# A gated token mixer on one core: the third branch's weight sums issued without marks, and three ring slots with six raw blocks instead of four with four

## The chip, the core and the metric

The kernel runs on one core of a Trainium2 chip. The metric is the device time of one execution in microseconds (us). Times of single instructions come from one profiled execution, and are counted from the start of its span.

## What is computed

One layer on an input x of 512 positions by 1024 channels, in float32:

```python
h = rmsnorm(x, norm_mix)
p = h @ w_in                                   # 1024 x 6144
u, v, bg, cg, xb, zc, gl = split(p)            # six of 512 columns, gl of 3 x 1024
ya = sgu(gelu(u), gelu(v), ...)                # 512 columns each
yb = bg * causal_dwconv(cg * xb, conv_b_w)
yc = pool_mixer(zc, pool_w, pool_scale)
g = sigmoid(gl)                                # three gates
merged = g[0] * (ya @ w_br_a) + g[1] * (yb @ w_br_b) + g[2] * (yc @ w_br_c)
x = x + merged @ w_o                           # output projection
h = rmsnorm(x, norm_ffn)
ag, av = split(causal_dwconv(h @ w_up, ffn_conv_w))   # 2 x 2816 columns
x = x + (silu(ag) * av) @ w_down
return rmsnorm(x, norm_f)
```

## The kernel before, in words

**Matrix products.** Each float32 factor is split into a high and a low part, and a product is three matmuls: high by high (L81), high by low (L82) and low by high (L83), each of 128 x 128 by 128 x 512. `st` are the activations, `mv` the weights.

**Weights: raw buffers, cuts, ring.** Weights come in blocks of 512 KB, 128 partitions by 1024 columns. SyncE loads a block into a *raw* buffer (L106); `Raws.cap` says how many raw buffers may be filled at a time: 4. The pool `rawp` has eight tiles of this size; four are raw buffers, and four hold two of the ring's slots. A block is then *cut* into a slot of the ring, `ring_hi` by ScalarE (L59, or L63 with the sign turned) and `ring_lo` by VectorE (L67, or L64). After the cut the raw buffer is free and the next load is issued. The ring `own` has four slots (0 and 1 in the pool `act`, 2 and 3 in `rawp`). `Pieces` counts the pieces: piece j goes into slot j modulo the number of slots, and `take` makes the pieces ahead by as many as there are slots:

```python
def take(self, n=1):
    i = self.taken
    self.taken += n
    self.ahead(i + len(self.slots))
    return [self.slots[k % len(self.slots)] for k in range(i, i + n)]
```

So the number of slots says how early a cut stands in the order of the engines' instructions, too. A planner that works with costs of its own then settles the order of the instructions on each engine; the chip runs each engine's list in that order.

**Branches and gates.** For i = 0, 1, 2 the program does `branch(i)`, the product of ya, yb or yc with its weights, and `gate(i)`, the product of h with the gate's 1024 columns, the sigmoid, and the weighing of the branch's result with it. Both are done with seven products of quarters instead of eight (m1 to m7, a scheme like Strassen's). A branch has 7 products of 12 matmuls (one piece each, 84 matmuls), a gate 7 products of 24 (two pieces each, 168). Banks of TensorE are named bx, bd, ba in a branch and gx, gd, ga in a gate; bx and bd are added to further after ScalarE has copied what they hold (L951, into `bm...`, `m...`). VectorE adds and subtracts copies and banks (L842, `tt`), ScalarE applies the sigmoid (L961). After the three come the output projection (`po`), the second norm, whose transposed result is split into `h2T_hi` and `h2T_lo`, and the up projection with blocks ug and uv (`pug`, `puv`), which uses the ring through a class of its own, `Cols`, with four slots.

**Sums of weights.** The seven products need sums of a weight's quarters. Branches 0 and 1 make them with VectorE in the raw buffers (`add_branch`, L178): all four blocks of the branch, b11, b12, b22, b21, lie in raw buffers until the fourth to seventh product. The gates and branch 2 have them made by `WeightSums`: DMAs issued by GpSimd copy quarters to four buffers t1 to t4 in memory (L146) and add other quarters to them (L151, a DMA that accumulates); the blocks are then loaded from there (`g_t`, `br_t`). The sums of gates 0 and 1 are issued early, after `v_center`, without conditions. Those of branch 2 (`last_branch_sums`, eight DMAs of 512 KB) and of gate 2 (`gate_sums[2]`, eight of 1 MB) are paced by *marks*: `next_sum`, called after a product, has ScalarE copy one column of the product's bank (`mark`, L936), GpSimd copy that (`passed`, L407), and GpSimd issue the next DMAs of the list `behind`. GpSimd's instructions keep the order written. There are eleven marks: seven in gate 0, one in branch 1 and three in gate 1.

Of the kernel before, what the change touches and what calls it, by code (L numbers as in the profile page):

```python
# [8 lines left out]
F32R = mybir.dt.float32r  # L9
# [5 lines left out]
P = 128  # L15
# [11 lines left out]
def trunk_kernel(  # L27
# [8 lines left out]
    rawp = ctx.enter_context(tc.tile_pool(name="rawp", bufs=8))  # L36
# [83 lines left out]
    raws = Raws()  # L120
# [14 lines left out]
    class WeightSums:  # L135
        def __init__(self, name, b11, b12, b21, b22):
            t1, t2, t3, t4 = self.t = [
                dram.tile([P, b11.shape[1], 528], F32, name=f"{name}_t{i + 1}")[:, :, :512] for i in range(4)]
            self.base = [(t1, b11), (t3, b12), (t2, b22), (t4, b21)]
            self.added = [(t1, b12), (t3, b22), (t2, t1), (t4, t2)]  # L140

            self.products = {"m1": b11, "m2": b21, "m3": b22, "m4": t4, "m5": t1, "m6": t2, "m7": t3}

# [215 lines left out]
    slots = own  # L359
# [38 lines left out]
    def quarters(half, c0):  # L398
        return [half(k)[:, :, c0 + 512 * h:c0 + 512 * h + 512] for k in range(2) for h in range(2)]

    gate_sums = [WeightSums(f"g{i}", *quarters(lambda k: w_in_v[:, 4 * k:4 * k + 4], 3072 + 1024 * i))
                 for i in range(3)]
    last_branch_sums = WeightSums("br2", *quarters(lambda k: w_br_q[2][k], 0))
# [228 lines left out]
        v_gelu(t)  # L632
    v_center()
    pool_waits_for(pw_raw, "begun")
    for sums in gate_sums[:2]:
        sums.copy()
        sums.add()

# [164 lines left out]

    pieces = Pieces(slots)
    for i in range(3):
        if i < 2:
            add_branch(f"br{i}", *quarters(lambda k: w_br_q[i][k], 0), pieces)
# [74 lines left out]
    sums = []  # L884
# [39 lines left out]
    nc.vector.tensor_scalar(nrstd1, rstd1, -1.0, None, op0=ALU.mult)  # L924


    behind = [lambda: last_branch_sums.copy()]
    behind += [lambda: last_branch_sums.add(1)] * 4
    behind += [lambda: gate_sums[2].copy(2)] * 2
    behind += [lambda: gate_sums[2].add(1)] * 4  # L930

    def next_sum(o):
        if behind:
            n = len(behind)
            mark = tiny(f"mark{n}", f"mark{n}")
            nc.scalar.copy(mark, o[:, 0:1])  # L936
            pool_waits_for(mark, f"passed{n}")
            behind.pop(0)()
# [89 lines left out]
    def branch(i, form):  # L1028
        c = [[act.tile([P, S], F32, tag=f"m{8 + 2 * t + h}" if i == 0 else f"x{t}{h}", name=f"c{i}{t}{h}")
              for h in range(2)] for t in range(NT)]  # L1030
        x = banks(f"bx{i}")
        product(x, form("a11"), 2, True)
        m1 = copies(0, f"bm1{i}", x)
        d = banks(f"bd{i}")
        product(d, form("s1"), 2, True)
        m5 = copies(1, f"bm5{i}", d)
        product(x, form("s2"), 2, False)
        if i > 0:
            next_sum(x[1])
        m16 = copies(2, f"bm16{i}", x)  # L1040
        a = banks(f"ba{i}")
        product(a, form("a12"), 2, True)
        for r in range(2):
            tt(c[r][0], a[r], m1[r], ALU.subtract)
        product(x, form("s3"), 2, False)
        for r in range(2):
            tt(c[2 + r][1], x[r], m5[r], ALU.add)
        product(d, form("s4"), 2, False)
        for r in range(2):
            tt(c[r][1], d[r], m16[r], ALU.add)  # L1050
        product(x, form("a22"), 2, False)
        for r in range(2):
            nc.scalar.mul(c[2 + r][0], x[r], -1.0)
        return c
# [16 lines left out]
    def prepare2():  # L1071
        if ready:
            to_channels(*ready.pop(0), 1, h2, xr)

    for h in range(2):
        o = {}

# [46 lines left out]
        down_sums.copy(1)  # L1124
        down_sums.add(1)

    n = pieces.done % len(slots)
    assert pieces.done == pieces.taken
    slots = slots[n:] + slots[:n]
    blocks = Cols(col_blocks[n_in:], slots)  # L1130

    def up_conv(o, c, i, name):
# [129 lines left out]
    pieces = Pieces(slots)  # L1262
# [19 lines left out]
    x = banks("dx")  # L1282
# [38 lines left out]
    f = [[bank(f"df{r}{i}") for i in range(len(cuts[r]))] for r in range(2)]  # L1321
# [44 lines left out]
```

## Time and profile before

| | |
|---|---|
| median of 3 runs | 739.06 us (738.57 to 740.81) |
| profiled execution | 736.67 us |
| its span | 734.9 us |
| TensorE busy in the span | 720.7 us, 98% |
| VectorE | 562.7 us, 77% |
| ScalarE | 370.6 us, 50% |
| GpSimd | 62.6 us, 9% |

The span is the stretch from the first to the last instruction in the profile; the rest of the execution's time, 1.77 us, lies outside it. Busy shares are means over the whole span. In the rows below PE is TensorE's matmuls, PEld its weight loads, DVE VectorE, ACT ScalarE, POOL GpSimd, and SPq SyncE's DMA queue. An engine's row may be busy while it is not at its peak.

### The profile page before, as it was taken

Reading aid. Unit: us, or ns where it says so; the run is one execution under the profiler, and the core shown is the slowest. Engines: PE = TensorE matmul, PEld = TensorE weight load, DVE = VectorE, ACT = ScalarE, POOL = GpSimd, SP = SyncE. Lnnn points to the kernel's source line nnn. Section 1 sums busy time; section 2 is a strip of 40 time slices with the busy share of each in tenths; the row PEclk is TensorE's granted clock in tenths of the full one; section 3 lists DMA queues with packets and bytes.
Section 4 is the critical chain, followed back from the end, with each engine's and each line's share of the span. In section 5 each row is a group of like instructions: output and inputs, shape, how many; then the busy total and the mean of one; then the engine's idle time right before and its main releaser. Section 6 shows DMA issues by size and latency. Waiting matters only on the chain.

```text
span 734.9 us, 8928 instructions
## 1 busy us (share of the span) xinstructions
PE 720.7 (98%) x3258; PEld 594.8 (81%) x3258; DVE 562.7 (77%) x836; ACT 370.6 (50%) x551; POOL 62.6 (9%) x93
## 2 busy tenths in 40 slices
PE   8999999999999998999999999999999999999996
PEld 5888888888877886888888888888888888888885
DVE  6889899889598687677556786766787776997674
ACT  4744144266675565664444443443444444965453
POOL 0041210001221100000012010100000000000110
PEclk9999999999999999999999999999999999999999
DMA  8649999737999996675228999999633232576652
GB/s 254 192 170 283 244 331 237 183 90 232 304 313 313 229 295 199 196 225 183 87 75 264 236 296 285 253 311 220 178 97 105 86 106 82 155 234 201 194 163 114
DMA packets 89211, 150.87 MB, mean 205 GB/s; under 512 B 4008, under 2 KB 39248, under 8 KB 89168
## 3 DMA queue, kind: packets, MB, share of 16 engines
q1 hardware_dynamic: 68607, 96.76, 41.7%
q0 software_dynamic: 19840, 52.43, 29.8%
q10 hardware_dynamic: 720, 1.11, 0.4%
q8 instruction: 25, 0.41, 0.2%
q14 instruction: 19, 0.15, 0.1%
HBM read 148.20 MB, written 54.53 MB: 276 GB/s over the span
## 4 chain that ended last, share of the span: by engine, by line
PE 93%; DVE 3%; DMA 2%; ACT 1%; issue 1%; SPq 0%; ACTq 0%
PE pug L83 5%; PE puv L83 5%; PE pug L81 5%; PE puv L81 5%; PE puv L82 5%; PE pug L82 5%; PE gx L82 3%; PE gx L81 3%; PE gx L83 3%; PE dx L83 2%; PE dx L82 2%; PE po L81 2%; PE dx L81 2%; PE po L83 2%; PE po L82 2%; PE gd L83 1%
## 5 line engine op out<-in xcount | busy, mean ns | idle before, releaser
L81 PE MATMUL pug<-h2T_hi,ring_hi 128*128 128x512 f32 x176 | 68.7, 390 | 0.0
L83 PE MATMUL pug<-h2T_hi,ring_lo 128*128 128x512 f32 x176 | 68.5, 389 | 0.0
L82 PE MATMUL puv<-h2T_lo,ring_hi 128*128 128x512 f32 x176 | 68.5, 389 | 0.0
L81 PE MATMUL puv<-h2T_hi,ring_hi 128*128 128x512 f32 x176 | 68.5, 389 | 0.0
L82 PE MATMUL pug<-h2T_lo,ring_hi 128*128 128x512 f32 x176 | 68.5, 389 | 0.0
L83 PE MATMUL puv<-h2T_hi,ring_lo 128*128 128x512 f32 x176 | 68.5, 389 | 0.0
L67 DVE TENSOR_TENSOR ring_lo<-raw_g_m,ring_hi 128x1024 fp32r<-128x1024 f32 x30 | 36.6, 1224 | 29.2 <-ACT ring_hi L59 29.1
L59 ACT CAST ring_hi<-raw_ug 128x1024 fp32r<-128x1024 f32 x22 | 23.3, 1057 | 47.4 <-PE pug L82 42.2
L67 DVE TENSOR_TENSOR ring_lo<-raw_uv,ring_hi 128x1024 fp32r<-128x1024 f32 x22 | 26.9, 1222 | 25.1 <-ACT ring_hi L59 25.1
L59 ACT CAST ring_hi<-raw_g_m 128x1024 fp32r<-128x1024 f32 x30 | 31.5, 1055 | 26.2 <-DMA raw_g_m<-in_w_in_dram 9.6
L67 DVE TENSOR_TENSOR ring_lo<-raw_d_m,ring_hi 128x1024 fp32r<-128x1024 f32 (+1 forms) x30 | 35.8, 1204 | 9.0 <-ACT ring_hi L59 8.9
L59 ACT CAST ring_hi<-raw_d_m 128x1024 fp32r<-128x1024 f32 (+1 forms) x30 | 29.5, 982 | 18.6 <-PE da L83 8.2
L82 PEld LDWEIGHTS puv<-h2T_lo,ring_hi 128*128 128x128 f32 x176 | 33.0, 188 | 6.9
L82 PEld LDWEIGHTS pug<-h2T_lo,ring_hi 128*128 128x128 f32 x176 | 33.0, 188 | 6.9
L83 PEld LDWEIGHTS pug<-h2T_hi,ring_lo 128*128 128x128 f32 x176 | 33.0, 188 | 6.9
L83 PEld LDWEIGHTS puv<-h2T_hi,ring_lo 128*128 128x128 f32 x176 | 33.0, 188 | 6.9
L81 PEld LDWEIGHTS puv<-h2T_hi,ring_hi 128*128 128x128 f32 x176 | 33.0, 188 | 6.9
L81 PEld LDWEIGHTS pug<-h2T_hi,ring_hi 128*128 128x128 f32 x176 | 33.0, 188 | 6.8
L67 DVE TENSOR_TENSOR ring_lo<-raw_ug,ring_hi 128x1024 fp32r<-128x1024 f32 x22 | 26.9, 1222 | 8.8 <-ACT ring_hi L59 8.7
L59 ACT CAST ring_hi<-raw_uv 128x1024 fp32r<-128x1024 f32 x22 | 23.2, 1056 | 19.1 <-PE puv L82 18.8
L1136 ACT ACTIVATE av<-av_y,colv 128x512 f32<-128x512 f32 x22 | 16.0, 727 | 27.9 <-DVE av_y L1134 26.9
L1136 ACT ACTIVATE ag<-ag_y,colv 128x512 f32<-128x512 f32 x22 | 15.8, 720 | 21.5 <-DVE ag_y L1134 21.5
(432 smaller groups left out, 2028.9 us busy)
## 6 DMA issues: line engine op xcount, KB each, us to landing
g_t<-in_w_in_dram POOLq DMA_DIRECT2D x18, 1024.0 KB, 13.2
d_t<-in_w_down_dram POOLq DMA_DIRECT2D x6, 2816.0 KB, 27.2
raw_g_m<-g_t SPq DMA_DIRECT2D x24, 512.0 KB, 4.2
raw_ug<-in_w_up_dram SPq DMA_DIRECT2D x22, 512.0 KB, 6.2
raw_uv<-in_w_up_dram SPq DMA_DIRECT2D x22, 512.0 KB, 5.1
raw_d_m<-d_t SPq DMA_DIRECT2D x20, 512.0 KB, 3.9
raw_g_m<-in_w_in_dram SPq DMA_DIRECT2D x18, 512.0 KB, 10.0
raw_d_m<-in_w_down_dram SPq DMA_DIRECT2D x15, 512.0 KB, 3.3
```

Source lines behind the costliest of these rows:

```text
L59: return keep(nc.scalar.copy(hi, src))
L67: return keep(nc.vector.tensor_tensor(lo, src, hi.bitcast(F32), op=ALU.subtract))
L81: keep(nc.tensor.matmul(o, st[0], mv[0], start=first, stop=False, **skip))
L82: keep(nc.tensor.matmul(o, st[0], mv[1], start=False, stop=False, **skip))
L83: keep(nc.tensor.matmul(o, st[1], mv[0], start=False, stop=last, **skip))
L1136: nc.scalar.activation(a, y, AF.Copy, scale=ffn_w(2, c))
```

## The change

1. `last_branch_sums` is issued right behind the sums of gates 0 and 1, without marks. The list `behind` holds only `gate_sums[2]`: one copy at each of gate 0's first four products, one addition at its last three and at gate 1's first; `branch` calls `next_sum` no more. `WeightSums` makes t1 to t4 in another order.
2. From branch 0 to gate 2 (and for the cuts ahead that reach beyond it) the ring has three slots, `slots[:3]`, and up to six raw buffers are filled. Before the output projection's loop the limit goes back to four. At the up projection a fourth slot is taken from `rawp` anew.

```diff
-            self.base = [(t1, b11), (t3, b12), (t2, b22), (t4, b21)]
-            self.added = [(t1, b12), (t3, b22), (t2, t1), (t4, t2)]
+            self.base = [(t1, b11), (t2, b22), (t3, b12), (t4, b21)]
+            self.added = [(t1, b12), (t2, t1), (t3, b22), (t4, t2)]
...
-    for sums in gate_sums[:2]:
+    for sums in gate_sums[:2] + [last_branch_sums]:
         sums.copy()
         sums.add()
...
-    pieces = Pieces(slots)
+    pieces = Pieces(slots[:3])
+    raws.cap = 6
...
-    behind = [lambda: last_branch_sums.copy()]
-    behind += [lambda: last_branch_sums.add(1)] * 4
-    behind += [lambda: gate_sums[2].copy(2)] * 2
+    behind = [lambda: gate_sums[2].copy(1)] * 4
     behind += [lambda: gate_sums[2].add(1)] * 4
...
-        if i > 0:
-            next_sum(x[1])
...
+    raws.cap = 4
     for h in range(2):
...
-    n = pieces.done % len(slots)
+    n = pieces.done % 3
...
-    slots = slots[n:] + slots[:n]
+    fourth = [rawp.tile([P, 1024], F32R, tag="raw", name=f"ring_{p}4") for p in ("hi", "lo")]
+    slots = slots[n:3] + slots[:n] + [fourth]
```

Three places in the order of the instructions. In the names, the number behind `ring_hi` or `ring_lo` is the slot's, `raw_br2_m5` is the block of branch 2's product m5, and the last number tells buffers apart.

First, ScalarE from the end of gate 1 to the first copies of branch 2, before:

```order
L63 ACTIVATE ring_hi2_79<-raw_br2_m1_0_2297 128x1024
L59 CAST ring_hi3_81<-raw_br2_m5_0_2317 128x1024
L961 ACTIVATE m1610_2231<-m1610_2231,n1_y_388 128x512
L961 ACTIVATE m1611_2232<-m1611_2232,n1_y_388 128x512
L59 CAST ring_hi0_75<-raw_br2_m6_0_2333 128x1024
L961 ACTIVATE s2110_2427<-gx10_2104,nrstd1_1441 128x512
L961 ACTIVATE s2111_2431<-gx11_2105,nrstd1_1441 128x512
L59 CAST ring_hi1_77<-raw_br2_m2_0_2357 128x1024
L59 CAST ring_hi2_79<-raw_br2_m7_0_2373 128x1024
L951 COPY bm120_2461<-bx20_2443 128x512
```

and after the change:

```order
L63 ACTIVATE ring_hi0_75<-raw_br2_m1_0_2269 128x1024
L961 ACTIVATE m1610_2219<-m1610_2219,n1_y_388 128x512
L961 ACTIVATE m1611_2220<-m1611_2220,n1_y_388 128x512
L59 CAST ring_hi1_77<-raw_br2_m5_0_2285 128x1024
L961 ACTIVATE s2110_2415<-gx10_2102,nrstd1_1449 128x512
L961 ACTIVATE s2111_2419<-gx11_2103,nrstd1_1449 128x512
L59 CAST ring_hi2_79<-raw_br2_m6_0_2305 128x1024
L59 CAST ring_hi0_75<-raw_br2_m2_0_2321 128x1024
L951 COPY bm120_2449<-bx20_2431 128x512
```

The cut of branch 2's second block (m5) stood ahead of the sigmoids m16; now it stands behind them. One cut (m7) that stood between the sigmoids s21 and the copies bm12 stands behind the copies now.

Second, TensorE at the end of branch 1's second product (bd) and in its third (bx, weights m6), before:

```order
L83 MATMUL bd11_1983<-ring_hi2_79,f12_11_lo_1770 128x512
L81 MATMUL bx10_1959<-ring_hi3_81,f12_10_hi_1748 128x512
L82 MATMUL bx10_1959<-ring_lo3_82,f12_10_hi_1748 128x512
L83 MATMUL bx10_1959<-ring_hi3_81,f12_10_lo_1749 128x512
L81 MATMUL bx11_1960<-ring_hi3_81,f12_10_hi_1748 128x512
L82 MATMUL bx11_1960<-ring_lo3_82,f12_10_hi_1748 128x512
L83 MATMUL bx11_1960<-ring_hi3_81,f12_10_lo_1749 128x512
L81 MATMUL bx10_1959<-ring_hi3_81,f12_11_hi_1769 128x512
```

and after:

```order
L83 MATMUL bd11_1985<-ring_hi1_77,f12_11_lo_1775 128x512
L81 MATMUL bx10_1963<-ring_hi2_79,f12_10_hi_1753 128x512
L81 MATMUL bx11_1964<-ring_hi2_79,f12_10_hi_1753 128x512
L81 MATMUL ba10_2028<-ring_hi0_75,fo_10_hi_1757 128x512
L82 MATMUL ba10_2028<-ring_lo0_76,fo_10_hi_1757 128x512
L83 MATMUL ba10_2028<-ring_hi0_75,fo_10_lo_1758 128x512
L81 MATMUL ba11_2029<-ring_hi0_75,fo_10_hi_1757 128x512
L82 MATMUL bx10_1963<-ring_lo2_80,f12_10_hi_1753 128x512
L83 MATMUL bx10_1963<-ring_hi2_79,f12_10_lo_1754 128x512
L82 MATMUL bx11_1964<-ring_lo2_80,f12_10_hi_1753 128x512
```

The first matmuls of the fourth product (ba) now stand between those of the third that read `ring_hi` (L81) and the first that reads `ring_lo` (L82): six matmuls are ahead of it.

Third, VectorE at the end of the output projection, where the last parts of the transposed norm are made and the up projection's first blocks are cut, before:

```order
L460 TENSOR_TENSOR xg114_3222<-tp114_3217,gain_139 128x512
L67 TENSOR_TENSOR h2T_lo_2908<-xg114_3222,h2T_hi_2907 128x4x128
L67 TENSOR_TENSOR ring_lo1_78<-raw_uv00_3099,ring_hi1_77 128x1024
L460 TENSOR_TENSOR xg124_3246<-tp124_3241,gain_139 128x512
L1093 TENSOR_TENSOR xr31_2898<-po13_3126,xr31_2898 128x512
L67 TENSOR_TENSOR ring_lo2_80<-raw_uv01_3103,ring_hi2_79 128x1024
L67 TENSOR_TENSOR h2T_lo_2908<-xg124_3246,h2T_hi_2907 128x4x128
L460 TENSOR_TENSOR xg134_3354<-tp134_3349,gain_139 128x512
```

and after:

```order
L460 TENSOR_TENSOR xg114_3210<-tp114_3205,gain_139 128x512
L67 TENSOR_TENSOR h2T_lo_2896<-xg114_3210,h2T_hi_2895 128x4x128
L67 TENSOR_TENSOR ring_lo0_76<-raw_ug01_3083,ring_hi0_75 128x1024
L460 TENSOR_TENSOR xg124_3234<-tp124_3229,gain_139 128x512
L1092 TENSOR_TENSOR xr31_2886<-po13_3110,xr31_2886 128x512
L67 TENSOR_TENSOR ring_lo1_78<-raw_uv00_3087,ring_hi1_77 128x1024
L67 TENSOR_TENSOR h2T_lo_2896<-xg124_3234,h2T_hi_2895 128x4x128
L67 TENSOR_TENSOR ring_lo4_3314<-raw_uv01_3119,ring_hi4_3313 128x1024
L460 TENSOR_TENSOR xg134_3344<-tp134_3339,gain_139 128x512
```

Ahead of xg13 there are three cuts in these rows instead of two: ug01, which was cut earlier, stands here now, and uv01 goes into the new slot 4.

## Rows read from the trace of the kernel before

**Rows 1.** The page of the profile: shares of the chain that ended last.
```profile
PE 93%; DVE 3%; DMA 2%; ACT 1%; issue 1%; SPq 0%; ACTq 0%
```

**Rows 2.** Busy time by windows (us from the span's start): branches and gates.
```profile
core 0: us, PE busy (x) PEld busy (x) DVE busy (x) ACT busy (x) POOL busy (x), PEclk, DMA share, GB/s
152.66:171.70 19.04, 19.04 (x86) 15.77 (x84) 16.13 (x22) 13.88 (x20) 0.00 (x0) 1.00 0.57 164
171.70:209.78 38.08, 38.08 (x170) 31.53 (x168) 27.21 (x37) 23.52 (x35) 11.82 (x16) 1.00 0.95 274
209.78:231.98 22.20, 19.94 (x86) 15.53 (x84) 19.81 (x26) 16.23 (x26) 4.23 (x5) 1.00 1.04 323
231.98:270.06 38.08, 38.08 (x170) 31.53 (x168) 27.75 (x35) 20.03 (x30) 4.01 (x6) 1.00 1.03 270
270.06:293.71 23.65, 20.94 (x86) 16.83 (x85) 19.08 (x23) 15.16 (x20) 0.00 (x0) 0.93 0.70 220
```

**Rows 3.** TensorE's waits: line waited for, us in total, times, longest us.
```profile
PE bx L81 <- ACT bm L951: 3.3, 2, 2.7
PE bx L81 <- DVE c L842: 1.7, 1, 1.7
```

**Rows 4.** Timeline of TensorE: start us, us, instruction, [idle before <-releaser].
```profile
216.93 0.50 PE L81 MATMUL bx<-ring_hi,f_hi 128*128 128x512 f32 x1 [0.54 <-ACT bm L951]
...
229.14 0.47 PE L81 MATMUL bx<-ring_hi,fo_hi 128*128 128x512 f32 x1 [1.72 <-DVE c L842]
...
278.37 0.65 PE L81 MATMUL bx<-ring_hi,f_hi 128*128 128x512 f32 x1 [2.71 <-ACT bm L951]
```

**Rows 5.** Timeline of SyncE's DMA issues between gate 0 and gate 1.
```profile
195.87 8.36 SPq L106 DMA_DIRECT2D raw_br_b<-in_w_br_b_dram  x4
218.53 5.57 SPq L106 DMA_DIRECT2D raw_g_m<-in_w_in_dram  x4
```

**Rows 6.** The tiles named raw_g_m: time from a load's issue to landing.
```profile
DMA to landing us min/median/max: 3.5/7.9/13.6
```

**Rows 7.** Timeline of ScalarE, then VectorE, around the pause at 229.14.
```profile
226.07 1.06 ACT L63 ACTIVATE ring_hi<-raw_g_m 128x1024 fp32r<-128x1024 f32 x1 [3.62 <-DMA raw_g_m<-in_w_in_dram]
...
227.16 1.23 DVE L64 SCALAR_TENSOR_TENSOR ring_lo<-raw_g_m,ring_hi 128x1024 fp32r<-128x1024 f32 x1 [2.26 <-ACT ring_hi L63]
228.31 1.28 DVE L842 TENSOR_TENSOR c<-bx,bm 128x512 f32<-128x512 f32 x2
```

**Rows 8.** Timeline of SyncE, ScalarE, then VectorE, ahead of the pause at 278.37.
```profile
261.47 1.84 SPq L106 DMA_DIRECT2D raw_br_m<-br_t  x2
...
270.04 1.05 ACT L59 CAST ring_hi<-raw_br_m 128x1024 fp32r<-128x1024 f32 x1 [4.37 <-PE gx L82]
...
277.74 1.19 ACT L951 COPY bm<-bx 128x512 f32<-128x512 f32 x2 [1.41 <-DVE c L842]
...
271.13 1.23 DVE L67 TENSOR_TENSOR ring_lo<-raw_br_m,ring_hi 128x1024 fp32r<-128x1024 f32 x1 [1.31 <-ACT ring_hi L59]
...
277.01 1.29 DVE L842 TENSOR_TENSOR c<-c,s 128x512 f32<-128x512 f32 x2
```

**Rows 9.** Timeline of GpSimd from 130 us, one cut of VectorE, one window.
```profile
132.77 1.02 POOL L151 DMA_DIRECT2D g_t<-g_t  x1 [12.56 <-issue]
...
205.09 0.89 POOL L151 DMA_DIRECT2D br_t<-br_t  x1 [3.54 <-issue]
...
205.62 1.23 DVE L64 SCALAR_TENSOR_TENSOR ring_lo<-raw_br_b,ring_hi 128x1024 fp32r<-128x1024 f32 x1 [0.58 <-ACT mark L936]
...
130.00:170.00 40.00, 40.00 (x178) 33.14 (x177) 33.96 (x45) 17.91 (x24) 1.02 (x1) 1.00 0.54 141
```

**Rows 10.** Timeline of VectorE, then TensorE, at the start of the up projection.
```profile
386.25 0.69 DVE L460 TENSOR_TENSOR xg<-tp,gain 128x512 f32<-128x512 f32 x1
387.73 0.68 DVE L67 TENSOR_TENSOR h2T_lo<-xg,h2T_hi 128x512 fp32r<-128x512 f32 x1
...
388.80 0.39 PE L82 MATMUL pug<-h2T_lo,ring_hi 128*128 128x512 f32 x1
```

## The prediction

> **What bounds the kernel now.** I read the page first: the chain that ended last lies 93% on TensorE [rows 1]. So only time in which TensorE stands still, or runs slower, can be won. To find it I took the windows of the stretch that the change touches [rows 2]. A gate has 168 matmuls, and both gates of the window take 38.08 us without idle time: 38.08 / 168 = 0.2267 us for a matmul, 12 x 0.2267 = 2.72 us for a piece (one ring slot's worth of weights). A branch has 84: branch 0 takes 19.04 us, which is 84 x 0.2267, so it loses nothing. Branch 1 takes 22.20, a loss of 3.16; branch 2 takes 23.65, a loss of 4.61. Together 7.77 us, all that this stretch can give back.
>
> The table of TensorE's waits says which they are [rows 3], and the timeline places them [rows 4]: 0.54 us at 216.93 for a copy that ScalarE makes of a bank (bm); 1.72 at 229.14 for a VectorE sum (c); 2.71 at 278.37 for bm again. The losses are larger than the waits, because the first matmuls after a pause come slower; in branch 2 the granted clock fell to 0.93 over the window [rows 2], and of its 4.61 us 1.90 are not the wait but matmuls at the lower of the two clock levels. A pause that goes takes this with it. I split branch 1's 3.16 into 2.00 at 229.14 and 1.16 at 216.93, in about the proportion of the waits with their slow matmuls.
>
> **Why the pauses stand there.** At 229.14: SyncE's loads of branch 1's four blocks end with the issue that starts at 195.87 and lasts 8.36, to 204.2; they hold all four raw buffers, and the next load (gate 1's first) is issued at 218.53, when the branch gives one back [rows 5]. It lands 3.5 to 13.6 us later, 7.9 in the median [rows 6]; ScalarE's cut of it waits for the DMA until 226.07, VectorE's other half of the cut follows at 227.16, and the two sums c, for which TensorE waits, are queued behind that at 228.31 [rows 7]. So a late weight block that TensorE itself needs only later stops VectorE, and VectorE stops TensorE.
>
> At 278.37: ScalarE's cut of branch 2's second block (m5) idles 4.37 us and starts at 270.04. The view names the gate's matmul, but that cut's slot was last read by gate 1's sixth product, which ended 5.44 us (two pieces) before the gate's end at 270.06. The load is the likelier cause: SyncE issued it at 261.47, when a fourth buffer came free. Behind this cut stand gate 1's last sigmoids, then VectorE's sums (idle 1.31 at 271.13, then at work without a break until 277.01 + 1.29), then the copies bm at 277.74, which waited 1.41 for VectorE [rows 8].
>
> **The change, part by part.**
> *Six raw buffers.* Two loads can be ahead while a branch holds its four blocks. Gate 1's first two loads would be issued right behind the last branch load, at about 201.5 to 204 us, where SyncE now stops [rows 5]. Even at 13.6 us to landing they are there at 217.6, 8.5 us before 226.07, where the first cut now starts. The cut's chain then no longer waits for DMA: 2.00 us won. Branch 2's second block is issued two loads earlier: two pieces, 5.44, less up to one piece by which the cuts come later with fewer slots, so at 256.0 to 258.8 instead of 261.47. At the median it has landed by 266.7 (at the longest by 272.4); it is needed one piece after the gate's end, 270.06 + 2.72 = 272.78, less a cut of 1.05 + 1.23: 270.50.
>
> *Three slots.* A slot is cut again when its piece's last matmul is over, and needed two pieces later: 5.44 us instead of 8.16. The cut is 1.06 on ScalarE and 1.23 on VectorE [rows 7], 2.29 in a row. With a pair of copies ahead on ScalarE (1.19) and a pair of sums ahead on VectorE (1.29) [rows 8] it is 4.77, still 0.67 under 5.44. I went through the order of both engines for every gate and branch with these durations and found the cuts ready 0.7 us or more before TensorE wants them. I cost it at nothing; the cover is those two pieces, and with it gone each gate product would lose what its chain is over 5.44.
>
> *Order of ScalarE.* With three slots the planner puts branch 2's second cut behind one pair of gate 1's sigmoids, and one cut fewer stands ahead of the copies bm (first place in the order above). By the same durations the copies end about 0.9 us before TensorE wants the bank. 4.61 us won: the wait and the matmuls at half clock.
>
> *Branch 1's third product (1.16 us).* Here the cut of this product comes later than before: ready at about 216.5, where TensorE could start at 215.3. But the new order of TensorE (second place) puts six matmuls that don't need its lower half ahead, 6 x 0.2267 = 1.36 us, to 216.6. The bm copies stand ahead of this cut now. I take all of 1.16 as won; if the cover fails, a wait of up to 1.2 comes in its place and nothing is won here.
>
> *The third branch's sums without marks.* Eight issues by GpSimd move to about 133 us on, right behind the one at 132.77, which lasts 1.02. In 130 to 170 us GpSimd is busy 1.02 us, the DMA engines 0.54, VectorE 33.96 of 40 [rows 9]: room for 8 x 1.02 = 8.2 us of issues and 8 half-megabyte transfers, and TensorE has no loss there. Three marks go with them (a one-column copy on ScalarE and one on GpSimd each). The same bytes leave the gates, whose DMA share is 0.95 to 1.03 [rows 2]; since TensorE waits nowhere in the gates, I count nothing for it, except that it makes the late landings less likely.
>
> The Trainium skill, SBUF — State Buffer, section "A bandwidth-pool intuition that's wrong", speaks against such a move: a GpSimd-issued DMA of about 620 ns takes about 3100 ns beside a VectorE copy, because the one locks the port of the other. The trace disagrees so far: the issue at 205.09 took 0.89 and reached into a VectorE cut at 205.62 that took 1.23, as the cut at 227.16 did with no issue beside it [rows 7, 9]. By the row the moved issues cost nothing, by the lock 8 x 1.02 = 8.2 us of VectorE time.
>
> *Back to four slots.* At the output projection four buffers again; its own first cuts come later, with other matmuls ahead of them, and I cost that at nothing (0 to 0.3). At the up projection the last of the four cuts goes into the new slot, and one more cut stands ahead of the last transposed block's chain on VectorE (third place in the order). A cut with its successor is 228.31 - 227.16 = 1.15 us [rows 7]. That chain is now xg at 386.25, h2T_lo at 387.73 to 388.41, and TensorE's first matmul with it at 388.80 [rows 10]: slack 0.39. 1.15 - 0.39 = 0.76, taken as 0.7 lost; 0 if the cut fits elsewhere, 1.2 if the slack does not help.
>
> **The sum.** The profiled execution took 736.67: - 2.00 - 1.16 - 4.61 + 0.70 = - 7.07, so 729.60. The median of the runs shown is 739.06, 2.39 above the profiled one; taken from it the forecast is 732.0. From no change a measurement of this kernel can tell about 0.3%, 2.2 us.
>
> **Rivals.**
> A, the forecast (0.60): the three pauses go, little is lost behind: 731 to 733.5.
>
> B (0.13): a pause stays or comes again one step later, since the sums and copies that TensorE waits for remain queued behind cuts. For it: the pause at 278.37 is a backlog of VectorE, and my margin there is 0.9 us. Against it: the load that started the backlog comes earlier. 732 + 2.0 = 734 where the one of 229.14 stays, 732 + 4.6 = 736.6 where the one of 278.37 does.
>
> P (0.04): the moved issues hold VectorE for 8.2 us in 130 to 170, where it has 40 - 33.96 = 6.04 to spare [rows 9]: 2.1 reach TensorE, 734.1. The row at 205.62 speaks against it. [...]
>
> C (0.13), within 0.3%: the change does not do what it says, because the blocks come no earlier. The six buffers are there, but a load waits for the queue: in the gates the DMA share is about 1 [rows 2], and branch 2's loads come one by one. Then the pauses at 229.14 and 278.37 move instead of going (+ 6.6), and 738.6 is left. Against it: the sums' bytes leave just these stretches.
>
> D (0.10), slower: three slots are too few in the gates. A product's copies and sums stand ahead of two cuts; where the chain is longer than 5.44, TensorE waits at every one of the 21 gate products. It decides when the 21 waits eat the gain of 7.07 and 2.2 more: 9.3 / 21 = 0.44 each, a chain of 5.88; at 6.0 it is 21 x 0.56 = 11.8, 743.8. For it: 4.77 is not far from it, and a further pair of sums (1.29) ahead would make 6.06. Against it: such a pair stands ahead of few cuts, and a matmul's last reader frees the slot without a wait.
>
> The Trainium skill, Perfetto Trace Analysis, section "Optimization Strategy", says that the same gap repeated on the engine that should be saturated can mean too few buffers. In the gates there is none with four slots (38.08 without idle time); D is that picture with three.
>
> **Chances and range.** Faster by over 0.3%, under 736.9: A, B and P, 0.77. Within: C, 0.13. Slower: D, 0.10. The range goes from 730.0 (all pauses gone, nothing lost at the up projection, 0.9 for the scatter of the runs) to 738.0, which takes in B, P and part of C; D and the rest of C are left out, somewhat under 0.2. A's own range is 731 to 733.5.
>
> **What would show it.** In the profile after: branches 1 and 2 at 19.0 to 19.4 us each with the granted clock at 1.00, gates at 38.08, no wait of bx for bm or c over 0.3; gate 1's first load issued before 205; br_t's eight issues between 133 and 165; one wait of up to 0.8 for h2T_lo at the up projection's start. Wrong would be: waits of gx or gd for the rings in the gates (D), VectorE cuts over 1.23 beside GpSimd's issues (P), a cut that waits for DMA at a branch's end (C).

## The result

The changed kernel takes 730.13 us (median of 4 runs, 729.91 to 730.40), the kernel before beside it 738.82 (737.35 to 740.81): a ratio of 0.9881, 95% interval 0.9857 to 0.9905. The forecast was 732.0, with a range of 730.0 to 738.0: the measured time lies 0.13 above the range's lower end, and under the 731 to 733.5 given for the forecast's own case A. The profiled execution took 730.32 us, 6.35 less than the profiled one of before; the forecast by profiled executions was 7.07 less. One execution of a later experiment, e10_slots, was disturbed (2589.01 us) and is left out of every median and ratio below.

The page after, its first line and the shares of the chain that ended last (to be read against [rows 1]):

```profile
span 728.5 us, 8915 instructions
...
PE 97%; DVE 1%; ACT 1%; DMA 1%; SPq 0%; issue 0%; ACTq 0%
```

The windows of branch 0, gate 0, branch 1, gate 1 and branch 2 after (columns as in [rows 2]: the window, its length and TensorE's busy time with instructions, then PEld, DVE, ACT, POOL, the granted clock, the DMA share and GB/s):

```profile
153.00:172.04 19.04, 19.04 (x85) 15.77 (x84) 15.09 (x21) 12.81 (x19) 0.89 (x1) 1.00 0.93 252
172.04:210.12 38.08, 38.08 (x169) 31.53 (x168) 29.73 (x39) 24.33 (x37) 5.39 (x11) 1.00 0.93 309
210.12:229.50 19.38, 19.36 (x86) 15.68 (x84) 19.02 (x24) 15.46 (x24) 2.61 (x3) 1.00 0.89 199
229.50:267.58 38.08, 38.08 (x170) 31.53 (x168) 30.38 (x40) 23.87 (x32) 1.57 (x2) 1.00 0.84 247
267.58:286.62 19.04, 19.04 (x86) 15.77 (x84) 15.37 (x18) 11.76 (x16) 0.00 (x0) 1.00 0.69 209
```

Branch 2 takes 19.04 us, as branch 0 does, at the full granted clock; branch 1 takes 19.38. Of the 7.77 us that the branches lost before, 0.34 are left. The gates are at 38.08 as before. All that the table of TensorE's waits still holds lies at the kernel's start (pauses as short as those left in branch 1 and at the up projection don't reach it); the rows for bx of [rows 3] are gone:

```profile
PE warm_ps L422 <- DVE warm L413: 1.6, 1, 1.6
PE tp L454 <- DMA x<-in_x_dram: 1.2, 1, 1.2
```

SyncE's timeline shows gate 1's first loads right behind the branch's four, where it stopped for 14 us before [rows 5]. The first two of these four issues start at 201.86 and 204.56; the other two, at 218.32 and 219.42, wait until branch 1 gives blocks back:

```profile
191.45 7.99 SPq L106 DMA_DIRECT2D raw_br_b<-in_w_br_b_dram  x4
201.86 17.93 SPq L106 DMA_DIRECT2D raw_g_m<-in_w_in_dram  x4
```

And on VectorE the two sums c for which TensorE waited stand ahead of the cut of gate 1's first block, not behind it [rows 7]:

```profile
224.33 1.29 DVE L844 TENSOR_TENSOR c<-bx,bm 128x512 f32<-128x512 f32 x2
225.53 1.22 DVE L64 SCALAR_TENSOR_TENSOR ring_lo<-raw_g_m,ring_hi 128x1024 fp32r<-128x1024 f32 x1
```

What was lost: at the up projection the last transposed block comes late. Its xg and h2T_lo on VectorE, and TensorE's matmuls there:

```profile
380.34 0.69 DVE L460 TENSOR_TENSOR xg<-tp,gain 128x512 f32<-128x512 f32 x1
381.82 0.68 DVE L67 TENSOR_TENSOR h2T_lo<-xg,h2T_hi 128x512 fp32r<-128x512 f32 x1
...
381.32 0.39 PE L83 MATMUL pug<-h2T_hi,ring_lo 128*128 128x512 f32 x1
381.73 0.73 PE L81 MATMUL pug<-h2T_hi,ring_hi 128*128 128x512 f32 x2
382.56 0.50 PE L82 MATMUL pug<-h2T_lo,ring_hi 128*128 128x512 f32 x1
```

Before, TensorE started a matmul each 0.23 us through this place; now it pauses ahead of 381.73 and of 382.56. From the first matmul of the up projection to the first of the down projection it takes 241.18 (the row stands below, at e5_fourth). Before, this window had no idle time:

```profile
382.54:623.00 240.46, 240.46 (x1065) 198.98 (x1064) 177.76 (x263) 102.58 (x147) 11.85 (x9) 1.00 0.71 194
```

The loss is 0.72 us, against 0.7 forecast.

By profiled executions: branches 7.77 - 0.34 = 7.43 won; 0.72 lost at the up projection, and 0.34 since branch 0 starts at 153.00 instead of 152.66 (the kernel's first loads came later in this execution). 7.43 - 0.72 - 0.34 = 6.37, as the spans say (734.9 - 728.5 = 6.4).

### The profile page after: what moved, and what is told of

The parts are those of the page before. It is cut to its first block, busy times and chain, and to the rows that moved or that the text cites. A ratio compares the mean times of both kernels' runs of the same rounds, so it can differ in the third digit from the quotient of the medians.

```text
span 728.5 us, 8915 instructions
## 1 busy us (share of the span) xinstructions
PE 719.0 (99%) x3258; PEld 593.8 (82%) x3258; DVE 563.5 (77%) x836; ACT 370.5 (51%) x548; POOL 58.8 (8%) x90
## 4 chain that ended last, share of the span: by engine, by line
PE 97%; DVE 1%; ACT 1%; DMA 1%; SPq 0%; issue 0%; ACTq 0%
PE puv L82 5%; PE puv L83 5%; PE puv L81 5%; PE pug L82 5%; PE pug L83 5%; PE pug L81 5%; PE gx L83 3%; PE gx L81 3%; PE gx L82 3%; PE dx L82 2%; PE dx L81 2%; PE dx L83 2%; PE po L81 2%; PE po L82 2%; PE po L83 2%; PE bx L81 2%
## 5 line engine op out<-in xcount | busy, mean ns | idle before, releaser
L82 PE MATMUL pug<-h2T_lo,ring_hi 128*128 128x512 f32 x176 | 68.6, 390 | 0.1
L81 PE MATMUL pug<-h2T_hi,ring_hi 128*128 128x512 f32 x176 | 68.6, 391 | 0.0
L82 PE MATMUL puv<-h2T_lo,ring_hi 128*128 128x512 f32 x176 | 68.5, 389 | 0.0
L81 PE MATMUL puv<-h2T_hi,ring_hi 128*128 128x512 f32 x176 | 68.5, 389 | 0.0
L82 PEld LDWEIGHTS pug<-h2T_lo,ring_hi 128*128 128x128 f32 x176 | 33.0, 188 | 7.3 <-DVE h2T_lo L67 0.5
L81 PEld LDWEIGHTS pug<-h2T_hi,ring_hi 128*128 128x128 f32 x176 | 33.0, 188 | 7.2 <-ACT h2T_hi L59 0.4
L81 PEld LDWEIGHTS puv<-h2T_hi,ring_hi 128*128 128x128 f32 x176 | 33.0, 188 | 6.9
L82 PEld LDWEIGHTS puv<-h2T_lo,ring_hi 128*128 128x128 f32 x176 | 33.0, 188 | 6.8
```

What stands on the lines that cost most here:

```text
L81: keep(nc.tensor.matmul(o, st[0], mv[0], start=first, stop=False, **skip))
L82: keep(nc.tensor.matmul(o, st[0], mv[1], start=False, stop=False, **skip))
```

## The experiments

Each ratio is to the kernel before, run beside it. Beside the changed kernel that one had a median of 738.82, beside e1_sums to e3_cap4 739.25, beside the later experiments 737.22: so compare kernels of different sets by their ratios, not by their medians. Ratios whose intervals overlap don't rank two kernels. A table of the windows comes first, since all kernels are read by it (us for the branch or gate; the first row is [rows 2]):

| kernel | branch 1 | gate 1 | branch 2 | the three | median of runs | ratio |
|---|---|---|---|---|---|---|
| before | 22.20 | 38.08 | 23.65 | 83.93 | 738.82 | |
| e0_again, the same kernel | 22.29 | 38.99 | 24.14 | 85.42 | 738.44 (one) | |
| e16_order_alone | 19.29 | 40.94 | 23.73 | 83.96 | 737.88 | 1.0005 (0.9990 to 1.0020) |
| e1_sums | 20.81 | 38.08 | 19.04 | 77.93 | 731.46 | 0.9905 (0.9868 to 0.9941) |
| e14_order | 19.12 | 39.23 | 19.04 | 77.39 | 729.17 | 0.9896 (0.9878 to 0.9914) |
| e17_slots_again / e10_slots | 19.40 | 38.08 | 19.04 | 76.52 | 730.13 | 0.9906 (0.9877 to 0.9935) |
| after | 19.38 | 38.08 | 19.04 | 76.50 | 730.13 | 0.9881 (0.9857 to 0.9905) |

The median beside e17_slots_again is that of e10_slots, the same kernel (five executions).

**e0_again: the kernel before, once more.** No edit.

> The kernel before, unchanged, profiled once more. The median gain (8.7 us) is larger than the difference of the two profiled runs (6.35). Theory A: the pauses at the ends of branch 1's products and in branch 2 depend on when loads land and differ from execution to execution, so this profile shows branch 1 and branch 2 with other losses than 3.16 and 4.61 us while the gates stay at 38.08. Theory B: the scatter lies elsewhere (the start, the down projection); then the branches lose 7.8 us again to within 0.3.

Theory A holds for the branches, not for the gates, which it wanted at 38.08: this execution, at 738.44 us, lost 3.25 in branch 1, 0.91 in gate 1 and 5.10 in branch 2, 9.26 where the first one lost 7.77. Its windows of branch 1, gate 1 and branch 2, and the longest wait of ScalarE at branch 2's start:

```profile
210.06:232.35 22.29, 19.95 (x85) 15.54 (x84) 19.94 (x26) 16.30 (x27) 4.24 (x5) 1.00 1.03 320
232.35:271.34 38.99, 38.40 (x169) 31.41 (x168) 27.54 (x35) 19.95 (x29) 4.08 (x6) 1.00 1.01 258
271.34:295.48 24.14, 19.97 (x86) 15.61 (x84) 19.32 (x24) 15.06 (x20) 0.00 (x0) 1.00 0.69 223
```

```profile
ACT ring_hi L59 <- DMA raw_br_m<-br_t: 6.0, 1, 6.0
```

This row settles what [rows 8] left open: ScalarE's cut of branch 2's second block waited 6.0 us for its load. The pauses depend on when loads land, so they differ from run to run: the execution profiled first had smaller ones than this one.

**e1_sums: the first part alone.**

```diff
-    for sums in gate_sums[:2]:
+    for sums in gate_sums[:2] + [last_branch_sums]:
-    behind = [lambda: last_branch_sums.copy()]
-    behind += [lambda: last_branch_sums.add(1)] * 4
-    behind += [lambda: gate_sums[2].copy(2)] * 2
+    behind = [lambda: gate_sums[2].copy(1)] * 4
```

(and the order of t1 to t4 and the call in `branch`, as in the change)

> Only the first part: the third branch's sums without marks and the eight marks; four slots and four raw buffers as before. Theory A (raw buffers and slots make the gain): the pause at the end of branch 1 for c stays (2.0 us), the one in its third product too (1.2), the one in branch 2 stays in whole or in part; 734.5 to 738 us. Theory B (the sums' traffic in the gates made the loads late): all pauses go, 730 to 732.

731.46 us: theory A's range is missed, and theory B comes out for two of three pauses. Windows of branch 1, gate 1 and branch 2, and what is left of TensorE's waits for bx:

```profile
210.32:231.13 20.81, 19.30 (x85) 15.69 (x84) 16.03 (x21) 13.68 (x22) 2.89 (x3) 1.00 0.92 216
231.13:269.21 38.08, 38.08 (x169) 31.54 (x168) 32.37 (x43) 24.54 (x34) 1.48 (x2) 1.00 0.82 233
269.21:288.25 19.04, 19.04 (x85) 15.77 (x84) 15.41 (x18) 11.74 (x16) 0.00 (x0) 1.00 0.67 207
```

```profile
PE bx L81 <- DVE c L842: 1.5, 1, 1.5
```

Branch 2 is whole, and so is branch 1's third product; only the pause for c stays. ScalarE waits for no DMA in gate 0 here, where it waited 6.2 us in all in the kernel before:

```profile
ACT ring_hi L59 <- DMA raw_g_m<-in_w_in_dram: 3.9, 2, 2.5
ACT ring_hi L63 <- DMA raw_g_m<-g_t: 1.2, 2, 1.1
ACT ring_hi L59 <- DMA raw_g_m<-g_t: 1.1, 1, 1.1
```

Beside the traffic, this edit takes three marks off ScalarE and GpSimd; no run separates the two.

**e2_ring: the second part alone** (three slots, `raws.cap = 6`, the fourth slot at the up projection; the sums as before).

> Only the second part: three slots, six raw buffers, the fourth slot at the up projection; the sums with eleven marks as before. Theory A (raw buffers and slots): the pauses go, branches 1 and 2 at 19.0 to 19.5 us, 730 to 731.5 us; up to 2 us more if the sums' traffic makes branch 2's second load late. Theory B (the sums' traffic): the pauses stay, 736 or more.

730.59 us (729.82 to 732.10), ratio 0.9897 (0.9853 to 0.9941): theory A. So either part alone brings nearly all: the two gains don't add.

**e3_cap4: the changed kernel without `raws.cap = 6`.**

```diff
     pieces = Pieces(slots[:3])
-    raws.cap = 6
```

> The changed kernel with four raw buffers instead of six from the branches to the output projection; the orders of ScalarE and TensorE at the two places are those of the changed kernel. Theory A (two loads ahead while a branch holds four blocks): gate 1's first load is issued only when branch 1 frees a block, the wait for c at branch 1's end is back with 1.5 to 2.5 us, 732 to 733.5 us, and up to 735 if branch 2's second load is late again. Theory C (the new order of the instructions from three slots made the gain, the buffers did not): no wait comes back, 730 us.

730.22 us, ratio 0.9886 (0.9851 to 0.9920): no difference from the changed kernel. But that is not yet theory C, because SyncE's loads come at the same times as with the limit at six:

```profile
201.64 3.07 SPq L106 DMA_DIRECT2D raw_g_m<-in_w_in_dram  x2
```

The lists of SyncE and of all other engines are the same in both kernels, row for row, so `raws.cap = 6` does nothing here. The limit counts while the program is written down, not on the chip: there a load waits until its tile of `rawp` is free. Four of the eight tiles were the slots 2 and 3; with slot 3 out of use six are left, whatever `cap` says. My experiment did not take the two buffers away.

**e10_slots and e17_slots_again: three slots alone** (e2_ring without `raws.cap = 6`; the lists of all engines are those of e2_ring, so these are further runs of one program).

> Three slots alone: four raw buffers, and the sums with eleven marks as before. Theory C (three slots give other orders on VectorE, ScalarE and TensorE, and these alone take the pauses away): branch 1 at 19.0 to 19.5 us, branch 2 at 19.0 to 19.5, 730 to 731 us. Theory D (orders mend only the pause for c at branch 1's end; the pause in branch 2 came from loads made late by the sums' traffic, and needs either the traffic gone or loads further ahead): ScalarE waits again for DMA in gate 0 and at branch 2's second block, branch 2 at 21 to 23.5 us, 732 to 735 us.

> Three slots alone once more (four raw buffers, the sums with eleven marks), for its profile, since the one taken first is of a disturbed execution. With a median of 730.7 the pauses must be gone. Theory C (orders alone): ScalarE and VectorE wait for DMA in gate 0 and at branch 2's second block as in the kernel before (2 to 4 us each), and TensorE does not. Theory F (the three-slot orders also bring the loads in earlier): no wait of ScalarE for DMA over 0.5 us in gate 0.

Five executions of e10_slots gave 729.39 to 732.34, median 730.13; e17_slots_again took 731.08. Its windows of branch 1, gate 1 and branch 2, and SyncE's first loads for gate 1:

```profile
210.90:230.30 19.40, 19.39 (x85) 15.69 (x84) 19.00 (x24) 15.49 (x25) 4.06 (x5) 1.00 1.04 325
230.30:268.38 38.08, 38.08 (x169) 31.53 (x168) 30.42 (x40) 23.98 (x34) 4.27 (x6) 1.00 1.08 299
268.38:287.42 19.04, 19.04 (x85) 15.77 (x84) 15.36 (x18) 11.77 (x16) 0.00 (x0) 1.00 0.76 241
```

```profile
202.64 3.07 SPq L106 DMA_DIRECT2D raw_g_m<-in_w_in_dram  x2
```

Theory F: ScalarE has no wait for DMA in gate 0 or at branch 2's start, though the DMA share is 1.04 and 1.08, as before. One edit, `slots[:3]`, frees the two buffers, and the loads are then ahead far enough for the sums' traffic not to matter. It changes the orders, too; no run has the one without the other.

**e14_order: four slots, four buffers, the sums early, and a place changed in VectorE's list.**

```diff
+        pieces.lead = 2 if i == 1 else 0
         c = branch(i, forms[i])
...
+            if name == "g1_m1_0":
+                tc.add_manual_dep(ins.ins, held[-1].ins.name, ..., reason="behind the sums c")
```

(`lead` has `take` cut only two pieces ahead in branch 1; `held[-1]` is the second of the sums c. ScalarE's and TensorE's orders are those of e1_sums. On VectorE the cut of gate 1's first block moves behind the sums c, and as a side effect that of its fourth goes ahead of a sum of 0.42 us.)

> Four slots and four raw buffers as before, the sums without marks, and one place of VectorE's list changed by hand: the cut of gate 1's first block (lower half) stands behind the two sums c of branch 1 instead of ahead of them; ScalarE's and TensorE's lists are those of the kernel with the sums alone. Theory C (that place made the pause at branch 1's end): the pause of 1.7 us that is left with the sums alone goes, branch 1 at 19.0 to 19.2 us, nothing is lost at the up projection's start, 729.0 to 729.8 us. Theory E (the pause goes only with an earlier load or a smaller ring): it stays, 731 to 732 us.

729.17 us: theory C by the time and by branch 1. Branch 1 and gate 1 (branch 2 is in the table):

```profile
210.21:229.33 19.12, 19.12 (x86) 15.69 (x85) 15.74 (x20) 11.54 (x19) 3.30 (x3) 1.00 0.87 180
229.33:268.56 39.23, 38.80 (x170) 31.28 (x168) 32.11 (x41) 26.20 (x36) 1.48 (x2) 1.00 0.86 255
```

The pause of branch 1 is gone with the load as late as before (SyncE issues it at 217.20; before at 218.53, in e1_sums at 216.41). But gate 1 takes 39.23: 1.15 of the 1.69 won in branch 1 are lost again there, where TensorE now waits three times for `ring_lo`, at 232.33, 237.97 and 255.05. And up to these sums c all engines have the lists of e1_sums; yet ScalarE waits 5.4 us for DMA in gate 0 here, and in e1_sums it did not wait. An earlier form, e13_order, had `take` cut two pieces ahead everywhere, for the output and down projections too; the down projection's last product takes four pieces at once, two of which aren't cut yet then, so that it reads weights of other blocks. It took 730.80 us, and nothing is read from it.

> Four slots and four raw buffers as before, the sums without marks, and one order of VectorE set by hand: the cut of gate 1's first block (lower half) behind the two sums c of branch 1 for which TensorE waited. Theory C (that place in VectorE's list made the pause at branch 1's end): that pause goes, branch 1 at 19.0 to 19.4 us, nothing is lost at the up projection's start, 729.0 to 729.9 us. Theory E (the pause needs the later load or the smaller ring to go): it stays with 1.5 to 2 us, 731 to 731.6 us as with the sums alone.

**e16_order_alone: the same edit in the kernel before.**

> The kernel before with that one place of VectorE's list alone: marks, four slots and four raw buffers as before. Theory C: only the pause at branch 1's end goes (2.0 us); the ones in branch 1's third product (1.2) and in branch 2 (4.6 and more) stay, since the loads stay late: 2 us under the kernel before, 735 to 737 us by the runs beside it. Theory E: no difference. A further case (the two later pauses hang on the first one, too): 730 us.

737.88 us, ratio 1.0005 (0.9990 to 1.0020): nothing. Theory C was right on that place, and wrong on the time and on branch 1's third product. Windows of branch 1, gate 1 and branch 2, and TensorE's waits:

```profile
209.90:229.19 19.29, 19.29 (x86) 15.69 (x84) 17.36 (x22) 13.28 (x22) 4.24 (x5) 1.00 1.03 334
229.19:270.13 40.94, 39.33 (x170) 31.30 (x168) 29.24 (x38) 21.58 (x31) 4.59 (x6) 1.00 1.01 263
270.13:293.86 23.73, 20.69 (x86) 16.68 (x85) 19.29 (x24) 15.16 (x20) 0.00 (x0) 0.93 0.70 227
```

```profile
PE bx L81 <- ACT bm L957: 3.0, 1, 3.0
PE gd L82 <- DVE ring_lo L67: 0.9, 2, 0.6
PE gd L81 <- ACT m L957: 0.6, 1, 0.6
PE gx L82 <- DVE ring_lo L67: 0.2, 1, 0.2
```

Branch 1 is 2.91 us shorter and gate 1 2.86 longer; the three windows take 83.96 instead of 83.93. Four waits in gate 1 took the place of the one removed. That fits loads that set the pace, with four buffers and the sums' traffic: SyncE issues branch 2's second block at 261.99 here and at 261.47 before, though branch 1 ended 2.8 us earlier. What goes in one place is then paid in the next.

Branch 1 won more than the 2.00 us of its end. Its third product lost 1.16 before, and the whole branch loses 0.25 here, though up to that product the lists of all engines are the same as before. What differs is when they ran: VectorE's cut of branch 1's first block, 4.16 us ahead of gate 0's end before (205.62 [rows 9]), stands 5.06 us ahead of it here.

```profile
204.84 1.22 DVE L64 SCALAR_TENSOR_TENSOR ring_lo<-raw_br_b,ring_hi 128x1024 fp32r<-128x1024 f32 x1
```

**e7_sums_order: the old order of t1 to t4 in the changed kernel.**

> The changed kernel with t1 to t4 made in the order of before (t1, t3, t2, t4). Nothing waits for these sums in the changed kernel by my reading: 729.9 to 730.5 us, branches 1 and 2 at 19.0 to 19.4 us. Rival (the block m6, which needs t2, would come late in gate 0 or branch 2): a wait of ScalarE for DMA in front of an m6 block, 731 or more.

729.92 us, ratio 0.9901 (0.9878 to 0.9923): no difference from the changed kernel that these runs can tell, and no new wait in TensorE's table.

**e5_fourth: the new slot first at the up projection.**

```diff
-    slots = slots[n:3] + slots[:n] + [fourth]
+    slots = [fourth] + slots[n:3] + slots[:n]
```

> The changed kernel with the slots of the up projection in another order: the new fourth slot comes first, so that its cut (ug00) waits for no matmul of the output projection. The number of cuts ahead of the last transposed block on VectorE is the same. Theory (that number makes the loss of 0.5 us at the up projection's start): it stays, 730.0 to 730.3 us. Rival (the slots of the output projection come free too late): it goes, 729.5 to 729.7 us.

729.42 us (729.02 to 729.94), ratio 0.9891 (0.9863 to 0.9918), against 729.91 to 730.40 of the changed kernel. The ratios' intervals overlap; it is the window that shows the loss gone. The window from the first matmul of the up projection to the first of the down projection, in the changed kernel and here:

```profile
375.50:616.68 241.18, 241.06 (x1066) 198.83 (x1064) 178.91 (x264) 103.07 (x148) 11.85 (x9) 1.00 0.70 191
```

```profile
375.82:616.28 240.46, 240.46 (x1065) 198.99 (x1064) 177.76 (x263) 102.35 (x147) 11.85 (x9) 1.00 0.71 194
```

My expectation was wrong on the order. With the free slot first, ug01's cut goes ahead of the last four blocks' chain, into a slot that is free earlier, and only two cuts stand between xg11 and xg13 on VectorE, as in the kernel before. So the edit changes the number that my theory wanted kept, and the result fits the theory and the rival alike. The changed kernel's trace speaks for the number: from 375.13 to 381.03 VectorE is at work there without a break, three cuts among it, so xg13 waits for what stands ahead of it and not for a slot.

**e6_two: two slots.**

> Two slots from the branches to the output projection, six raw buffers. A slot comes free when its piece is over and is needed one piece later, 2.72 us; the cut alone is 2.29 us. Where a pair of copies or sums stands ahead of it the chain is 3.5 to 4.8. Theory (a slot must cover the cut's chain): TensorE waits for ring_lo in nearly every gate product with up to 2 us, 0.5 to 1.5 us on average over the 21 gate and 21 branch products and 4 more pieces: 750 to 790 us. Rival (cuts are hidden however short the ring is, as with three slots): within 2 us of the changed kernel.

740.38 us, ratio 1.0040 (1.0025 to 1.0056), 10.25 over the changed kernel's median: the theory's direction, and its size too large by far. Gate 0 and branch 1:

```profile
172.65:211.83 39.18, 39.01 (x169) 31.21 (x168) 29.71 (x39) 25.42 (x38) 5.36 (x11) 1.00 0.93 299
211.83:233.69 21.86, 20.16 (x85) 15.45 (x84) 20.03 (x25) 14.71 (x23) 3.18 (x3) 1.00 0.95 234
```

Gate 0 loses 1.1 us, 0.16 for each of its products on the mean, instead of 0.5 to 1.5. It does so at three places only (181.24, 190.10 and 198.32), each time ahead of the first matmul of a piece that reads `ring_lo`: most cuts still fit under the one piece of 2.72. The branches lose up to 2.5 against the changed kernel.

## Why the prediction was right, point by point

**The pauses and their sum.** The losses of 3.16 and 4.61 us were read right, and all but 0.34 of them went. What the prediction had wrong is which part of the change takes them away.

**"Six raw buffers", 2.00 us.** The mechanism came as described: gate 1's first load is issued at 201.86 and the second at 204.56; the second takes 8.6 us to land (the trace has no landing for the first), and ScalarE's cuts of both, from 224.26 on, wait for no DMA. What I had not seen is that it hangs on the third slot alone (e3_cap4, e17_slots_again), and that a second thing changed at this place: the cut stands behind the sums c in VectorE's list. e14_order shows that this order removes the pause with the load still late, though most of what it wins is lost again in gate 1. Whether the early load would do so with the old order was not tried; nor was a ring of three with only four buffers.

**The pause in branch 2, 4.61 us.** I had put its start down to a late load and its end to ScalarE's order, and cost the order. The load is the cause: e0_again names it (6.0 us), and in e1_sums, where SyncE issues this load at 257.45 instead of 261.47, the pause is gone with that cut still ahead of the sigmoids, as in the order before. In the changed kernel both reasons are gone: the load is issued at 251.08, earlier than the 256.0 to 258.8 I gave; whether the new order alone would do it with a late load no run shows.

**Branch 1's third product, 1.16 us.** The cover of six matmuls worked (the first read of `ring_lo` follows at 217.25), but I took the wrong thing as the cause and left out a small wait. In e1_sums, with TensorE's order of before, this pause is gone as well, together with ScalarE's waits for DMA in gate 0; that points to loads that were late there and set ScalarE and VectorE back. e16_order_alone shows that no new order is needed: with the lists of before the pause shrinks from 1.16 to about 0.25 us, in an execution in which VectorE reaches branch 1's first cut 0.9 us sooner. Waits for DMA in gate 0 alone don't tell it: e14_order has 5.4 us of them and loses 0.08 in branch 1, its cut standing 5.92 us ahead of the gate's end. What is left of it after, 0.34, is a pause ahead of the first matmuls, not of those with `ring_lo`:

```profile
215.34 0.39 PE L83 MATMUL bd<-ring_hi,f_lo 128*128 128x512 f32 x1
215.75 0.73 PE L81 MATMUL bx<-ring_hi,f_hi 128*128 128x512 f32 x2
216.32 0.40 PE L81 MATMUL ba<-ring_hi,fo_hi 128*128 128x512 f32 x1
...
217.25 0.40 PE L82 MATMUL bx<-ring_lo,f_hi 128*128 128x512 f32 x1
```

**The sums without marks.** "I count nothing for it" was the step that failed in its reason, though not in the sum: alone it brings a ratio of 0.9905, the ring alone 0.9897 and 0.9906. That the sum came out with nothing for it was luck: each part takes away nearly the same pauses, so the one left out didn't show. A reason that the traces give is that loads land sooner without the marked sums. In the kernel before the two loads issued from 243.17 on took 12.4 to 13.6 us to land, and the same two in e1_sums 9.4 to 10.5:

```profile
DMA to landing us min/median/max: 12.4/13.0/13.6
DMA to landing us min/median/max: 9.4/9.9/10.5
```

With four in flight a block comes each 13.0 / 4 = 3.25 us by the first row and each 9.9 / 4 = 2.48 by the second (estimates from these rows), and TensorE uses one each 2.72. These are among the slowest loads: over gate 0, branch 1 and the start of gate 1 the medians are 10.0 and 9.6, nearer to each other. The moved issues cost nothing where they went; the last row is the window that holds them:

```profile
125.85 3.22 POOL L146 DMA_DIRECT2D br_t<-in_w_br_c_dram  x4
141.72 1.06 POOL L151 DMA_DIRECT2D br_t<-in_w_br_c_dram  x1 [12.66 <-DMA br_t<-in_w_br_c_dram]
...
149.48 1.40 POOL L151 DMA_DIRECT2D br_t<-in_w_br_c_dram  x1
155.18 0.89 POOL L151 DMA_DIRECT2D br_t<-br_t  x1 [4.30 <-issue]
...
125.85:156.07 30.22, 30.22 (x135) 25.04 (x134) 23.80 (x33) 7.65 (x10) 7.15 (x9) 1.00 0.97 244
```

They begin at 125.85, earlier than I said, and TensorE has no idle time there. VectorE's operation at 141.78, begun during the issue at 141.72, took 1.23 us; the same operation at 143.53, with no issue beside it, 1.22. Rival P is out. The Trainium skill, SBUF — State Buffer, section "A bandwidth-pool intuition that's wrong", has its figures, about 620 ns alone and about 3100 ns beside a VectorE copy, for a GpSimd-issued DMA. By the trace VectorE makes no copy beside these issues, and the cut at 205.62 that the prediction set against these figures is none either: all of them take two inputs. So no run here tests that case, and "the trace disagrees so far" said too much.

**Three slots cost nothing (D).** The gates stay at 38.08. With two slots the loss begins, so the ring was one step from its end: 5.44 us of cover are enough, 2.72 are not. The Trainium skill, Perfetto Trace Analysis, section "Optimization Strategy", says that the same gap repeating on the engine that should be saturated can mean that there isn't room for the next tile. e6_two comes near that picture in the gates (39.18 instead of 38.08, three pauses ahead of `ring_lo` in gate 0), and three slots don't show it.

**The up projection, 0.7 us.** 0.72, by the mechanism named.

**The rest.** 732.0 was 1.9 above the measured 730.13. The step from the profiled execution to the median took the losses as equal in all runs; they vary (9.26 in e0_again), so the median gain (8.69) is larger than that of the two profiled executions (6.35). The measured time is in the range by 0.13 us, and that is luck: by the terms named for the range's lower end (nothing lost at the up projection, 0.9 for the scatter) it would be 732.0 - 0.7 - 0.9 = 730.4. Between the fastest and the slowest run lie 0.5 us after, but 2.2 in e1_sums, 2.3 in e2_ring, 3.0 in e10_slots and 3.5 before: with one part alone some executions still take 2 to 3 us more than others, and no profile here shows where.

So the gain has, as far as these runs go, one cause with two cures. Loads came late, since four buffers were few for landings of up to 13.6 us under the sums' traffic; ScalarE and VectorE, whose lists run in order, passed the lateness on to TensorE. For the pause in branch 2 and the one at branch 1's end the late load stands in the rows; for branch 1's third product the runs show only that it hangs on the time, not on the order. Moving the sums cures it but for one cut's place (three windows at 77.93 us); a ring of three, which frees two buffers and changes the orders, cures it whole (76.52); both together are the same there (76.50), with the least scatter. By their ratios the three can't be told apart. The lowest medians are those of e14_order (729.17) and e5_fourth (729.42), 0.7 to 1.0 under the changed one, but not by their ratios. For e5_fourth the windows show 0.72; for e14_order they show 0.89 more than the changed kernel in the three windows.

## What to carry to other kernels

Where an engine waits for a short operation, ask what stands ahead of that operation in its engine's list, and whether that in turn waits for a load; if so, the load, more than the operation, is the thing to move. Removing one such pause can move the loss to the next stage: sum the windows behind it before counting a gain (e16_order_alone). And two cures of one cause don't add, so a change in several parts says little about each until each has run alone.

## What was not expected of the hardware

Where the trace has a landing for them, gate loads of the same 512 KB took from 3.5 to 13.6 us to land in the kernel before and from 3.6 to 10.9 in the changed one. The DMA share doesn't tell the two apart: in gate 0 it is 0.95 before [rows 2] and 0.93 after, while the last three loads of that gate's blocks took 8.1 to 11.8 us to land before and 5.4 to 7.0 after. What about the marked sums makes loads late stays open. And a limit in the program on loads in flight had no effect on when they were issued: with `cap` at 4 or 6 the loads came at 201.64 and 201.86 us; the free tiles of the pool decided.
